# A mixture-of-experts block on one core: weights read in longer pieces, a different assignment of hidden units, and one buffer moved between two stages

## The chip, the cores and the metric

The kernel runs on one core of one Trainium2 chip. Times are device microseconds of one execution. Three runs of the kernel before took 1500.37, 1500.58 and 1503.2 us; the median is 1500.58 us. In the texts PE is TensorE, PEld its weight load, DVE VectorE, ACT ScalarE, POOL GpSimd, SP SyncE (which issues the weight transfers).

## The reference, cut to what matters

One decoder block on 512 tokens of 1024 channels. A recurrence and a windowed attention come first; their sum goes through an output projection. The part that the change touches follows:

```python
x = x + g1 * (merged @ w_out)                       # output projection and residual
h2 = rms_norm(x, norm2_gain) * (1 + sc2) + sh2
x = x + g2 * moe_ffn(h2, ...)                       # 32 experts, each token goes to 4

# per expert e, for the tokens xb that chose it
hu = xb @ w_up[e] + b_up[e]                         # w_up[e]: 1024 x 2048
x_glu = minimum(hu[:, ::2], 7)                      # even columns
x_lin = clip(hu[:, 1::2], -7, 7)                    # odd columns
act = x_glu * sigmoid(1.702 * x_glu) * (x_lin + 1)
y = act @ w_down[e] + b_down[e]                     # w_down[e]: 1024 x 1024
```

All is float32. Hidden unit h of an expert comes from columns 2h and 2h+1 of w_up and meets row h of w_down.

## The kernel before, in words

**Precision.** Matrix products run in float16 with each weight split into a high part (scaled and rounded, written by ACT in line 341) and a low part (what is left, computed by DVE in line 346), and three matmuls per product (high x high, low x high, high x low). A split takes a tile of 128 x 2048 float32 from a staging slot and writes two float16 halves into another slot.

**The slots.** All weights pass through a ring of slots, each 8 KB per partition. `NS` = 9 stand from the start (named slot). When the output projection begins, `NSB` = 5 more come (slotb); when the experts begin, and the projection's own tiles are given back, `NSC` = 4 more (slotc). A free slot is taken either by `pump`, which issues the next weight transfer on SP in a fixed order, or by `hl_take` for the output of a split. `free` and `hl_give` put slots back and pump again. The low part of a split is the last reader of a staged tile, so it decides when a weight slot comes free.

**The experts.** For each of 32 experts the ring brings eight tiles of w_up (`q_up`, rows 128k to 128k+127, 8 KB per row) and four of w_down (`q_dn`: 256 rows as two blocks of 128, so that one partition receives rows p and 128+p, 4 KB each). The eight up tiles and three of the four down tiles are split; the last down tile is used as float32. `split_up` reads the up tile with `p (f g) -> p g f`, g = 2: all even columns, then all odd ones, so that the innermost step of the read is 2 elements (8 bytes). The halves are written contiguously. `up_k` then takes 16 blocks of 128 columns (8 of the gated part, 8 of the linear part), each three matmuls against the gathered tokens `xg` of one k. `swiglu` forms the activation, `down_j` multiplies it with the down tiles, `finish` scales by gate and adds the rows to the output by an indirect DMA on POOL.

**Order.** In the expert loop the instructions of PE, ACT and DVE stay in the order in which they are written. `ahead(i)` issues the splits up to `LOOK` = 6 tiles ahead of the one being multiplied, as long as slots are free. Work of expert e's down product, expert e+1's up product and expert e+2's gather is woven together.

**The output projection.** For each of four tiles of 128 tokens, `logits` computes the projection, adds it to the residual input `x1`, forms the router's logits and writes x1 out (a DMA issued on POOL, line 983). Before, all four x1 tiles have a buffer of their own and are loaded on ACT's queue ahead of the loop (line 945).

**The table.** `overflow_table` computes how many experts got more tokens than one pass takes, and which; the loop behind the experts (line 1401) uses it and runs no pass here. Before, it is issued as one piece in the last turn of the expert loop.

Of the kernel before, what the change touches and what calls it, by code (L numbers as in the profile page):

```python
# [23 lines left out]
NT = 4  # L24
# [17 lines left out]
def block_body(tc, x, c, positions, w_ada, b_ada, norm1_gain, w_in, lower_bound_logits, hg_norm_gain,  # L42
# [19 lines left out]
    with top:  # L62
# [41 lines left out]
        def dview(ap, off, dims):  # L104
            return bass.AP(tensor=ap.tensor, offset=ap.offset + off, ap=dims)
# [54 lines left out]

        def q_dn(e, j):
            queue(("dn", e, j), lambda t: SP.dma_start(
                t.rearrange("p (k f) -> p k f", k=2),
                dview(w_down, (e * 1024 + 256 * j) * 1024, [[1024, 128], [128 * 1024, 2], [1, 1024]])))

        for g in range(4):
            q_ada1(g, 0)
# [772 lines left out]

        x1s, xas, rss = {}, {}, {}

        for t in range(NT):
            x1s[t] = wk.tile([128, D], F32, name=f"x1_{t}")
            A.dma_start(x1s[t], x2[128 * t:128 * t + 128, :])

        def logits(t, pieces):
# [92 lines left out]

        def bias_up():
            st = ready.pop(("bup",))
            src = st[:32, :].rearrange("p (f g) -> p g f", g=2)
            bk = sd_bank()
            for m in range(16):
                T.transpose(bk[:, 32 * m:32 * m + 32], src[:, m // 8, 128 * (m % 8):128 * (m % 8) + 128],
                            ident[:32, :32])
            A.activation(bu.rearrange("p e m -> p m e"), bk.rearrange("p (m e) -> p m e", m=16), AF.Copy, scale=SU)
            free(st)

# [4 lines left out]
            free(st)  # L1055

        def split_up(e, k, later=None):
            split(("up", e, k), 2048, later=later, view_in=lambda t: t.rearrange("p (f g) -> p g f", g=2),
                  view_hi=lambda t: t.rearrange("p (g f) -> p g f", g=2))

        order = []
        for e in range(NEX + 1):
# [25 lines left out]
        def select0(t0, t1):  # L1088
            V.tensor_tensor(sel0[:, t0:t1], iota_c[:, None, :C].to_broadcast([128, t1 - t0, C]),
                            pos[:, t0:t1, 0:1].to_broadcast([128, t1 - t0, C]), op=OP.is_equal)  # L1090

        for t in range(NT):
            if t == NT - 1:
                select0(0, NT - 1)
            logits(t, ((0, D),) if t < NT - 1 else LAST)
            pre(t + 1)
            if t < NT - 1:
                choose(t)
                make_h2(t)
                gates(t)  # L1100
# [84 lines left out]

        def up_k(hl, k, xg):
            for f in range(16):
                o = pu[f // 4][:, C * (f % 4):C * (f % 4) + C]
                for n, (pa_, pw) in enumerate(PASSES):
                    T.matmul(o, lhsT=hl[:, 2048 * pw + 128 * f:2048 * pw + 128 * f + 128], rhs=xg[:, pa_, k, :],  # L1190
                             start=False, stop=(k == KT - 1 and n == 2), skip_group_check=True)

        def swiglu(act, act32, read=None):
# [61 lines left out]

        NB = 32

        def overflow_table():

            cb = pse.tile([128, 512], F32, name="gb", bufs=2)  # L1260
            for t in range(NT):
                T.matmul(cb[:, :NE], lhsT=onesb, rhs=Mb[:, t, :], start=(t == 0), stop=(t == NT - 1))
            cnt = moe.tile([128, NE], F32, name="cnt")
            V.tensor_copy(cnt, cb[:, :NE])
            nbk = moe.tile([128, NE], F32, name="nbk")
            V.tensor_scalar(nbk, cnt, float(C), None, op0=OP.is_gt)
            q = 2
            while C * q < S:
                V.scalar_tensor_tensor(nbk, cnt, float(C * q), nbk, op0=OP.is_gt, op1=OP.add)
                q += 1  # L1270
            cum = moe.tile([128, NE], F32, name="cum")
            one_e = moe.tile([128, NE], F32, name="one_e")
            V.memset(one_e, 1.0)
            V.tensor_tensor_scan(cum, one_e, nbk, 0.0, op0=OP.mult, op1=OP.add)
            nblk = moe.tile([128, 2], I32, name="nblk")
            V.tensor_copy(nblk[:, 0:1], cum[:, NE - 1:NE])
            slot = hl_take()[0]
            cmpt = slot[:, :NB * NE].rearrange("p (b e) -> p b e", b=NB)
            V.tensor_tensor(cmpt, iota_c[:, :NB, None].to_broadcast([128, NB, NE]),
                            cum[:, None, :].to_broadcast([128, NB, NE]), op=OP.is_gt)  # L1280
            eix = moe.tile([128, NB], F32, name="eix")
            V.tensor_reduce(eix, cmpt, axis=AX.X, op=OP.add)
            eixi = moe.tile([128, NB], I32, name="eixi")
            V.tensor_scalar(eix, eix, float(NE - 1), None, op0=OP.min)
            V.tensor_copy(eixi, eix)
            beg = moe.tile([128, NB], F32, name="beg")

            V.tensor_sub(cum, cum, nbk)
            V.tensor_tensor(cmpt, iota_e[:, None, :].to_broadcast([128, NB, NE]),
                            eix[:, :, None].to_broadcast([128, NB, NE]), op=OP.is_equal)  # L1290
            V.tensor_mul(cmpt, cmpt, cum[:, None, :].to_broadcast([128, NB, NE]))
            V.tensor_reduce(beg, cmpt, axis=AX.X, op=OP.add)
            V.tensor_sub(beg, iota_c[:, :NB], beg)
            V.tensor_scalar(beg, beg, float(C), None, op0=OP.mult)
            hl_give(slot)
            return nblk, eix, eixi, beg

        def aux_of(e):
            return lambda t: aux[:, t, e, :]
# [29 lines left out]
        def rest():  # L1329

            for b in range(4):
# [2 lines left out]
                        next(prep, None)  # L1334
                up_bias(bu[:, 1], b)

        i = 0
        for e in range(NEX + 1):
            if e < NEX:
                prep = nexts.pop(e + 1, iter(()))  # L1340
                xg = state[e][0]
                for k in range(8):
                    ahead(i)
                    if e > 0 and k in PICK_AT:
                        next(prep, None)
                    up_k(hlmap[("up", e, k)], k, xg)
                    hl_done(("up", e, k))
                    i += 1
                    if e == 0 and k == 4:
                        for t in range(NT):  # L1350
                            T.matmul(gbs[3][:C, 4 * C:4 * C + 3], lhsT=sel0[:, t, :], rhs=aux[:, t, 0, :], start=False,
                                     stop=(t == NT - 1), skip_group_check=True)
                        slots_of(gbs[3][:C, 4 * C:4 * C + 3], gate, idx)
                        hl_give(sel0slot)
                        A.activation(gate[:, 3:4], bu[:, 0, 0:1], AF.Silu)
                lows = []
                ahead(i, lows)
                acts[e] = new_act()
                swiglu(*acts[e], read=rest if e == 0 else None)
                for low in lows:  # L1360
                    low()
                for _ in prep:
                    pass
                if e + 2 < NEX:
                    nexts[e + 2] = prepare(e + 2)
                    next(nexts[e + 2])
            if e == NEX:
                tables = overflow_table()
            if e > 0:
                _, gate, idx = state.pop(e - 1)  # L1370
                down_bias(E64[:, e - 1:e])
                for j in range(4):
                    ahead(i)
                    key = ("dn", e - 1, j)
                    if j < 2 and e < NEX - 1:
                        up_bias(bu[:, e + 1], 2 * j)
                        up_bias(bu[:, e + 1], 2 * j + 1)
                    if j >= 3:
                        down_j(ready[key], j, *acts[e - 1])
                        free(ready.pop(key))  # L1380
                    else:
                        down_j(hlmap[key], j, *acts[e - 1])
                        hl_done(key)
                    i += 1
                finish(gate, idx)
                acts.pop(e - 1)
# [14 lines left out]
        with tc.For_i(0, nreg, 1) as it:  # L1401
# [27 lines left out]
            for k in range(8):  # L1429
# [1 line left out]
                free_slots.rotate(-1)  # L1431
                SP.dma_start(stt, wup[ds(er, 1)].rearrange("o k f -> (o k) f")[128 * k:128 * k + 128, :])
                slot, hl = hl_take()
                src = stt.rearrange("p (f g) -> p g f", g=2)
                hi, lo = (hl[:, :2048].rearrange("p (g f) -> p g f", g=2),
                          hl[:, 2048:].rearrange("p (g f) -> p g f", g=2))
                A.activation(hi, src, AF.Copy, scale=SW)
                V.scalar_tensor_tensor(lo, src, SW, hi, op0=OP.mult, op1=OP.subtract)
                up_k(hl, k, xg)
# [5 lines left out]
            for j in range(4):  # L1445
                stt = free_slots[0]
                free_slots.rotate(-1)
                SP.dma_start(stt.rearrange("p (k f) -> p k f", k=2),
                             wdn[ds(er, 1)].rearrange("o (j k p) f -> p (o j) k f", j=4, k=2)[:, j])
                if j >= 3:  # L1450
                    down_j(stt, j, act, act32)
                    continue
# [9 lines left out]
        'w_hg_branch', 'q_norm_gain', 'k_norm_gain', 'attn_sinks', 'w_attn_branch', 'w_out', 'norm2_gain',  # L1462
        'w_router', 'b_router', 'w_up', 'b_up', 'w_down', 'b_down']
_OUTS = [((1, 512, 1024), 'float32')]
NSB, NSC = 5, 4
LOOK = 6
NHX = 6
SW_AT = {0: 1, 1: 2, 2: 2, 5: 4, 6: 3, 7: 3, 8: 3, 9: 3, 10: 3, 11: 3, 12: 3, 13: 3}
HG_AT = {9: 1, 10: 1, 11: 1, 12: 1, 13: 1, 14: 1, 15: 1, 16: 1, 17: 1}
# [25 lines left out]
```

## Time and profile before

| | us |
|---|---|
| median of three runs | 1500.58 |
| the profiled execution, its own time | 1501.85 |
| its span in the trace | 1500.1 |
| PE, DVE, ACT busy | 1402.3, 1299.1, 1053.5 |
| the experts, from the first up product to the last | 447 to 1463 |
| output projection | about 380 to 447 |

The profile is of one execution. Busy shares are averages over unlike stages, so the stage of the experts, two thirds of the span, is read by itself. A row that groups instructions gives their count, their busy time in total and the mean of one; a row of a stretch gives each engine's busy time in it, the granted TensorE clock (1.00 is full speed), the share of time that the 16 DMA engines were busy, and their rate.

### The profile page before, as it was taken

Reading aid. Unit: us, or ns where it says so; the run is one execution under the profiler, and the core shown is the slowest. Engines: PE = TensorE matmul, PEld = TensorE weight load, DVE = VectorE, ACT = ScalarE, POOL = GpSimd, SP = SyncE. Lnnn points to the kernel's source line nnn. Section 1 sums busy time; section 2 is a strip of 40 time slices with the busy share of each in tenths; the row PEclk is TensorE's granted clock in tenths of the full one; section 3 lists DMA queues with packets and bytes.
Section 4 is the critical chain, followed back from the end, with each engine's and each line's share of the span. In section 5 each row is a group of like instructions: output and inputs, shape, how many; then the busy total and the mean of one; then the engine's idle time right before and its main releaser. Section 6 shows DMA issues by size and latency. Waiting matters only on the chain. (4 is left out here: it accounts for less than half of the span.)

```text
span 1500.1 us, 41126 instructions
## 1 busy us (share of the span) xinstructions
PE 1402.3 (93%) x18200; PEld 1035.1 (69%) x18200; DVE 1299.1 (87%) x1457; ACT 1053.5 (70%) x1024; POOL 358.4 (24%) x82
## 2 busy tenths in 40 slices
PE   3979999999977999999999999999999999999994
PEld 2536567444557887788877888777887777888771
DVE  6876677777898999999999999999998899999885
ACT  4555424622548888888888888888887888888770
POOL 1020000010110233312433344203344333344400
PEclk9999999999989999999999999999999999999997
DMA  9832321376758999999999999999999999999971
GB/s 314 266 97 85 113 56 57 130 251 239 289 213 312 372 397 404 406 403 402 410 396 408 409 404 410 387 403 396 397 408 385 402 384 407 390 397 408 386 291 18
DMA packets 113521, 476.44 MB, mean 318 GB/s; under 512 B 10718, under 2 KB 35387, under 8 KB 80539
## 3 DMA queue, kind: packets, MB, share of 16 engines
q1 hardware_dynamic: 106160, 458.78, 77.8%
q0 software_dynamic: 5440, 12.72, 3.9%
q8 instruction: 144, 2.36, 0.6%
q10 hardware_dynamic: 1738, 2.27, 0.4%
q14 instruction: 39, 0.31, 0.1%
HBM read 463.22 MB, written 14.70 MB: 319 GB/s over the span
## 5 line engine op out<-in xcount | busy, mean ns | idle before, releaser
L1245 POOL DMA_INDIRECT out_dram<-y,idx x32 | 325.1, 10159 | 725.0 <-DVE y L1253 685.1
L1190 PE MATMUL pu<-xg,slot 128*128 128x96 f16 x10224 | 463.2, 206 | 10.5 <-issue 7.0
L1190 PEld LDWEIGHTS <-slot 128*128 128x128 f16 x10224 | 446.0, 98 | 28.6 <-issue 23.7
L346 DVE SCALAR_TENSOR_TENSOR slot<-slot,slot 128x2048 f16<-128x2048 f32 (+1 forms) x120 | 271.4, 2271 | 37.2 <-ACT slot L341 36.9
L341 ACT ACTIVATE slot<-slot 128x2048 f16<-128x2048 f32 (+1 forms) x120 | 242.2, 2031 | 79.1 <-DVE slot L346 24.6
L346 DVE SCALAR_TENSOR_TENSOR slot<-slotb,slot 128x2048 f16<-128x2048 f32 x101 | 227.7, 2282 | 8.2 <-ACT slot L341 7.9
L346 DVE SCALAR_TENSOR_TENSOR slot<-slotc,slot 128x2048 f16<-128x2048 f32 x97 | 219.7, 2283 | 12.6 <-ACT slot L341 12.4
L341 ACT ACTIVATE slot<-slotc 128x2048 f16<-128x2048 f32 x97 | 201.5, 2104 | 31.4 <-DMA slotc<-in_w_up_dram 9.9
L1241 PEld LDWEIGHTS <-act 128*96 128x96 f16 x1152 | 140.4, 124 | 115.5 <-issue 16.0
L341 ACT ACTIVATE slot<-slotb 128x2048 f16<-128x2048 f32 x101 | 197.4, 1957 | 32.0 <-PE pu L1190 11.4
L1241 PE MATMUL pd<-slot,act 128*96 128x512 f16 x924 | 206.4, 380 | 0.0
L701 PE MATMUL mm<-hT,slot 128*128 128x512 f16 x672 | 151.4, 381 | 0.0
L701 PEld LDWEIGHTS <-slot 128*128 128x128 f16 x672 | 65.5, 98 | 77.8 <-issue 2.9
L1150 PE MATMUL gb<-sel,h 128*128 128x96 f16 x1984 | 106.3, 208 | 11.7 <-ACT xg L1157 8.0
L1150 PEld LDWEIGHTS <-h 128*128 128x128 f16 x1984 | 92.4, 98 | 12.4 <-issue 10.3
L1190 PE MATMUL pu<-xg,slotb 128*128 128x96 f16 x2064 | 95.8, 206 | 4.2 <-issue 2.3
L1190 PEld LDWEIGHTS <-slotb 128*128 128x128 f16 x2064 | 90.7, 98 | 8.1 <-issue 7.1
L785 POOL DMA_DIRECT2D mdram<-mr x8 | 4.7, 591 | 270.0 <-DVE mr L779 207.0
L1233 PE MATMUL pd<-slot,act 128*96 128x512 f32 x144 | 64.7, 592 | 0.0
L1157 ACT ACTIVATE xg<-gb 128x384 f16<-128x384 f32 x124 | 59.1, 477 | 1.6 <-PE gb L1150 1.4
L1183 ACT ACTIVATE pu<-bu 128x384 f32<-128x384 f32 x128 | 57.0, 477 | 0.0
L346 DVE SCALAR_TENSOR_TENSOR slotb<-slot,slotb 128x2048 f16<-128x2048 f32 x20 | 45.8, 2289 | 11.6 <-ACT slotb L341 11.5
(339 smaller groups left out, 1634.9 us busy)
## 6 DMA issues: line engine op xcount, KB each, us to landing
slotc<-in_w_up_dram SPq DMA_DIRECT2D x116, 1024.0 KB, 19.4
slot<-in_w_up_dram SPq DMA_DIRECT2D x110, 1024.0 KB, 18.1
slotb<-in_w_down_dram SPq DMA_DIRECT2D x98, 1024.0 KB, 21.6
slotb<-in_w_up_dram SPq DMA_DIRECT2D x30, 1024.0 KB, 16.7
slot<-in_w_down_dram SPq DMA_DIRECT2D x20, 1024.0 KB, 22.5
slot<-in_w_in_dram SPq DMA_DIRECT2D x16, 1024.0 KB, 5.3
slot<-in_w_ada_dram SPq DMA_DIRECT2D x16, 1024.0 KB, 5.4
slotc<-in_w_down_dram SPq DMA_DIRECT2D x10, 1024.0 KB
```

Of the source, the lines that this page charges most:

```text
L341: A.activation(hi, src, AF.Copy, scale=SW)
L346: V.scalar_tensor_tensor(lo, src, SW, hi, op0=OP.mult, op1=OP.subtract)
L701: T.matmul(bk, lhsT=hl[:, o:o + 128], rhs=hT[:, ph, k, :], start=(k == 0 and n == 0), stop=(k == KT - 1 and n == 2))
L785: G.dma_start(mdram[q:q + 1, 512 * u:512 * u + 512], m)
L1150: T.matmul(bk[:, C * k:C * k + C], lhsT=h2[:, part, t, 128 * kk:128 * kk + 128], rhs=sel[:, t, :], start=(k == 0 and t == 0), stop=(t == N ...
L1157: A.activation(xg[:, part, 4 * u:4 * u + 4, :].rearrange("p k c -> p (k c)"), bk[:, :4 * C], AF.Copy)
L1183: A.activation(pu[i][:, :4 * C].rearrange("p (m c) -> p m c", m=4), b[:, 4 * i:4 * i + 4, None].to_broadcast([128, 4, C]), AF.Copy)
L1190: T.matmul(o, lhsT=hl[:, 2048 * pw + 128 * f:2048 * pw + 128 * f + 128], rhs=xg[:, pa_, k, :], start=False, stop=(k == KT - 1 and n == 2), ...
L1233: T.matmul(pd[u][:C, :], lhsT=act32[:, k - 4, :], rhs=w[:, o:o + 512], start=False, stop=(k == KT - 1))
L1241: T.matmul(pd[u][:C, :], lhsT=act[:, pa_, k, :], rhs=w[:, c0:c0 + 512], start=False, stop=False)
L1245: G.indirect_dma_start(out=out2, out_offset=bass.IndirectOffsetOnAxis(ap=idx[:n, :1], axis=0), in_=y[:n, :], in_offset=None, bounds_check= ...
```

## The change

1. `q_dn` reads 256 rows of w_down so that partition p receives rows 2p and 2p+1 of the block: one piece of 8 KB for each partition instead of two of 4 KB.
2. Hidden units must then meet these rows. The split of an up tile reads `p (f r) -> p r f` with r = 4: four passes of 512 elements, the innermost step being 4 elements (16 bytes). `up_k` picks its 128-column blocks accordingly, and so does `bias_up`.
3. x1 has two buffers. Tiles 0 and 1 are loaded ahead of their use as before; the load of tile t+1 is written ahead of the projection of tile t, on ACT's queue.
4. `NSB` goes from 5 to 6 and `NSC` from 4 to 3: one slot is there from the output projection on instead of from the experts on.
5. The table is a generator in three pieces, run in the turns of experts 6, 8 and 10 behind k = 3; each of the two later pieces borrows a ring slot while it runs.
6. In the first and the last turn with an up product, splits are no longer issued ahead between the up product and swiglu.

```diff
         def q_dn(e, j):
             queue(("dn", e, j), lambda t: SP.dma_start(
-                t.rearrange("p (k f) -> p k f", k=2),
-                dview(w_down, (e * 1024 + 256 * j) * 1024, [[1024, 128], [128 * 1024, 2], [1, 1024]])))
+                t, dview(w_down, (e * 1024 + 256 * j) * 1024, [[2048, 128], [1, 2048]])))
...
-        for t in range(NT):
-            x1s[t] = wk.tile([128, D], F32, name=f"x1_{t}")
+        def load_x1(t):
+            x1s[t] = wk.tile([128, D], F32, name="x1", bufs=2)
             A.dma_start(x1s[t], x2[128 * t:128 * t + 128, :])
...
         def split_up(e, k, later=None):
-            split(("up", e, k), 2048, later=later, view_in=lambda t: t.rearrange("p (f g) -> p g f", g=2),
-                  view_hi=lambda t: t.rearrange("p (g f) -> p g f", g=2))
+            split(("up", e, k), 2048, later=later, view_in=lambda t: t.rearrange("p (f r) -> p r f", r=4),
+                  view_hi=lambda t: t.rearrange("p (r f) -> p r f", r=4))
...
+        load_x1(0)
         for t in range(NT):
             if t == NT - 1:
                 select0(0, NT - 1)
+            if t < NT - 1:
+                load_x1(t + 1)
             logits(t, ((0, D),) if t < NT - 1 else LAST)
...
         def up_k(hl, k, xg):
             for f in range(16):
+                cb = 512 * (2 * (f % 2) + f // 8) + 128 * (f % 8 // 2)
                 o = pu[f // 4][:, C * (f % 4):C * (f % 4) + C]
                 for n, (pa_, pw) in enumerate(PASSES):
-                    T.matmul(o, lhsT=hl[:, 2048 * pw + 128 * f:2048 * pw + 128 * f + 128], rhs=xg[:, pa_, k, :],
+                    T.matmul(o, lhsT=hl[:, 2048 * pw + cb:2048 * pw + cb + 128], rhs=xg[:, pa_, k, :],
...
                     up_k(hlmap[("up", e, k)], k, xg)
                     hl_done(("up", e, k))
+                    if k == 3 and e in TABLE_AT:
+                        next(table)
...
                 lows = []
-                ahead(i, lows)
+                if 0 < e < NEX - 1:
+                    ahead(i, lows)
...
-            if e == NEX:
-                tables = overflow_table()
...
-NSB, NSC = 5, 4
+NSB, NSC = 6, 3
 LOOK = 6
+TABLE_AT = (6, 8, 10)
```

The order of instructions moves in two places that the prediction speaks of. The first is ACT in the output projection. Before, where `x_1_2862` to `x_3_2866` are the residual tiles of t = 1 to 3, ACT has no load among its work here:

```order
L1021 ACTIVATE gt,gs<-gt 128x4
L971 ACTIVATE xat<-sd 128x512
L963 ACTIVATE sqt,rs<-x_1_2862 128x1024
L971 ACTIVATE xat<-sd 128x512
L1004 ACTIVATE h_2220<-xa 128x1024
L1021 ACTIVATE gt,gs<-gt 128x4
```

Now, with `x_2899` the tile of t = 1 and `x_3170` that of t = 3 (lines are one lower):

```order
L1020 ACTIVATE gt,gs<-gt 128x4
L962 ACTIVATE sqt,rs<-x_2899 128x1024
L970 ACTIVATE xat<-sd 128x512 x2
L944 DMA x_3170<-in_x_dram 128x1024
L1003 ACTIVATE h_2220<-xa 128x1024
L1020 ACTIVATE gt,gs<-gt 128x4
```

The load of the fourth tile now stands in ACT's stream between the transposes' evictions of tile 1 and the cast of its h2; it waits for the write-out of tile 1, whose buffer it takes.

The second place is DVE behind the last split (`slot_71` before, `slot_64` now). Before, the table stands between the result of expert 30 and that of expert 31:

```order
L346 SCALAR_TENSOR_TENSOR slot_71<-slotc_3544,slot_71 128x2048
L1253 SCALAR_TENSOR_TENSOR y<-pd_3469,gate,g2row 96x512
L1253 SCALAR_TENSOR_TENSOR y<-pd_3470,gate,g2row 96x512
L1264 COPY cnt<-gb 128x32
L1266 TENSOR_SCALAR nbk<-cnt 128x32
L1269 SCALAR_TENSOR_TENSOR nbk<-cnt,nbk 128x32 x4
```

Now the two results stand one behind the other:

```order
L345 SCALAR_TENSOR_TENSOR slot_64<-slot_70,slot_64 128x2048
L1256 SCALAR_TENSOR_TENSOR y<-pd_3471,gate,g2row 96x512
L1256 SCALAR_TENSOR_TENSOR y<-pd_3472,gate,g2row 96x512
L1256 SCALAR_TENSOR_TENSOR y<-pd_3471,gate,g2row 96x512
L1256 SCALAR_TENSOR_TENSOR y<-pd_3472,gate,g2row 96x512
```

The table's instructions have left the end of DVE's stream; the same instructions stand in the turns of experts 6, 8 and 10.

## Rows read from the trace of the kernel before

**Rows 1.** The head of the page: busy time and share of each engine

```profile
PE 1402.3 (93%) x18200; PEld 1035.1 (69%) x18200; DVE 1299.1 (87%) x1457; ACT 1053.5 (70%) x1024; POOL 358.4 (24%) x82
```

**Rows 2.** Busy time by stretch: length, then each engine, TensorE clock, DMA share, GB/s

```profile
447.00:1463.00 1016.00, 988.90 (x15823) 799.79 (x15823) 950.35 (x790) 851.07 (x729) 322.25 (x30) 1.00 0.99 392
500.00:1440.00 940.00, 923.00 (x14603) 741.22 (x14601) 885.87 (x737) 791.61 (x679) 320.83 (x29) 1.00 1.01 399
```

**Rows 3.** What the weight queue waited for: us in total, times, longest

```profile
SPq L158 <- DVE slot L346: 258.6, 111, 8.1
```

**Rows 4.** DMA issues, from the page: KB each, us from issue to landing

```profile
slotc<-in_w_up_dram SPq DMA_DIRECT2D x116, 1024.0 KB, 19.4
...
slotb<-in_w_down_dram SPq DMA_DIRECT2D x98, 1024.0 KB, 21.6
```

**Rows 5.** Lines by form on DVE, low half of a split: busy us, mean ns, idle before

```profile
L346 DVE SCALAR_TENSOR_TENSOR slot<-slotb,slot 128x2048 f16<-128x2048 f32 x101 | 227.7, 2282 | 8.2 <-ACT slot L341 7.9
L346 DVE SCALAR_TENSOR_TENSOR slot<-slotc,slot 128x2048 f16<-128x2048 f32 x97 | 219.7, 2283 | 12.6 <-ACT slot L341 12.4
```

**Rows 6.** Lines by form on ACT, high half of a split

```profile
L341 ACT ACTIVATE slot<-slotc 128x2048 f16<-128x2048 f32 x97 | 201.5, 2104 | 31.4 <-DMA slotc<-in_w_up_dram 9.9 <-ACT slot L341 7.3 <-issue 6.3
L341 ACT ACTIVATE slot<-slotb 128x2048 f16<-128x2048 f32 x101 | 197.4, 1957 | 32.0 <-PE pu L1190 11.4 <-DMA slotb<-in_w_down_dram 8.7 <-DMA slotb<-in_w_up_dram 6.0
```

**Rows 7.** Lines by form on DVE: line 635 by length, and a sum of contiguous rows

```profile
L635 DVE TENSOR_TENSOR hf<-hf 128x512 f32<-128x512 f32 x2 | 1.4, 688 | 0.0
...
L635 DVE TENSOR_TENSOR hf<-hf 128x256 f32<-128x256 f32 x2 | 1.2, 624 | 0.0
...
L960 DVE TENSOR_TENSOR x<-x,xa 128x256 f32<-128x256 f32 x2 | 0.8, 414 | 0.0
```

**Rows 8.** Lines by form on DVE: one-operand reductions

```profile
L555 DVE TENSOR_REDUCE sst<-scores 128x8 f32<-128x2048 f32 x3 | 6.9, 2284 | 0.1
...
L1025 DVE TENSOR_REDUCE ge<-oh 128x32 f32<-128x128 f32 x4 | 1.5, 365 | 0.0
...
L1282 DVE TENSOR_REDUCE eix<-slotb 128x32 f32<-128x1024 f32 x1 | 1.2, 1220 | 0.0
```

**Rows 9.** Lines by form on ACT: two evictions of 512 elements

```profile
L971 ACT ACTIVATE xat<-sd 128x512 f16<-128x512 f32 x7 | 4.2, 597 | 8.9 <-PE sd L968 8.9
...
L1048 ACT ACTIVATE bu<-sd 128x512 f32<-128x512 f32 x1 | 1.0, 1033 | 4.9 <-PE sd L1046 4.9
```

**Rows 10.** Timeline of the end: start us, us, engine, line, operation, idle before

```profile
1471.63 0.17 DVE L1264 COPY cnt<-gb 128x32 f32<-128x32 f32 x1
...
1480.23 0.18 DVE L1294 TENSOR_SCALAR beg<-beg 128x32 f32<-128x32 f32 x1
...
1484.45 0.75 DVE L1253 SCALAR_TENSOR_TENSOR y<-pd,gate,g2row 96x512 f32<-96x512 f32 x1 [4.04 <-PE pd L1233]
```

**Rows 11.** Timeline of the output projection: writes of two tiles, and one ACT row

```profile
392.55 0.55 POOL L983 DMA_DIRECT2D out_dram<-x  x1 [9.45 <-DVE x L960]
...
410.70 0.56 POOL L983 DMA_DIRECT2D out_dram<-x  x1 [3.33 <-DVE gt L1023]
...
416.44 1.06 ACT L1004 ACTIVATE h<-xa 128x1024 f16<-128x1024 f32 x1 [3.77 <-DVE xa L1003]
```

**Rows 12.** DMA issues: those writes

```profile
out_dram<-x POOLq DMA_DIRECT2D x4, 512.0 KB, 6.3
```

**Rows 13.** Busy time in stretches of 2 us

```profile
438.00:440.00 2.00, 1.19 (x8) 0.60 (x8) 1.50 (x10) 0.59 (x3) 0.47 (x1) 0.50 0.99 418
474.00:476.00 2.00, 2.00 (x29) 2.00 (x27) 1.54 (x4) 1.28 (x3) 0.00 (x0) 0.50 0.80 324
482.00:484.00 2.00, 1.38 (x33) 1.38 (x34) 2.00 (x3) 1.77 (x2) 0.00 (x0) 1.00 0.42 86
```

**Rows 14.** Timeline of PE: the same gather at two clocks

```profile
463.64 1.52 PE L1150 MATMUL gb<-sel,h 128*128 128x96 f16 x32
473.16 2.72 PE L1150 MATMUL gb<-sel,h 128*128 128x96 f16 x32 [8.00 <-ACT xg L1157]
```

More of the change, by code (lines that the diff above doesn't have):

```diff
@@ L1042, in bias_up @@
             st = ready.pop(("bup",))
-            src = st[:32, :].rearrange("p (f g) -> p g f", g=2)
+            src = st[:32, :].rearrange("p (f r) -> p r f", r=4)
             bk = sd_bank()
             for m in range(16):
-                T.transpose(bk[:, 32 * m:32 * m + 32], src[:, m // 8, 128 * (m % 8):128 * (m % 8) + 128],
-                            ident[:32, :32])
+                k = m % 8
+                T.transpose(bk[:, 32 * m:32 * m + 32], src[:, 2 * (k % 2) + m // 8, 128 * (k // 2):128 * (k // 2) + 128], ident[:32, :32])
             A.activation(bu.rearrange("p e m -> p m e"), bk.rearrange("p (m e) -> p m e", m=16), AF.Copy, scale=SU)
@@ L1256, in block_body @@
         NB = 32
+        tables = []
         def overflow_table():
@@ L1276, in overflow_table @@
             V.tensor_copy(nblk[:, 0:1], cum[:, NE - 1:NE])
+            yield
             slot = hl_take()[0]
@@ L1282, in overflow_table @@
             V.tensor_reduce(eix, cmpt, axis=AX.X, op=OP.add)
+            hl_give(slot)
             eixi = moe.tile([128, NB], I32, name="eixi")
@@ L1288, in overflow_table @@
             V.tensor_sub(cum, cum, nbk)
+            yield
+            slot = hl_take()[0]
+            cmpt = slot[:, :NB * NE].rearrange("p (b e) -> p b e", b=NB)
             V.tensor_tensor(cmpt, iota_e[:, None, :].to_broadcast([128, NB, NE]),
@@ L1295, in overflow_table @@
             hl_give(slot)
-            return nblk, eix, eixi, beg
+            tables.extend((nblk, eix, eixi, beg))
+            yield
         def aux_of(e):
@@ L1335, in rest @@
                 up_bias(bu[:, 1], b)
+        table = overflow_table()
         i = 0
@@ L1433, in block_body @@
                 slot, hl = hl_take()
-                src = stt.rearrange("p (f g) -> p g f", g=2)
-                hi, lo = (hl[:, :2048].rearrange("p (g f) -> p g f", g=2),
-                          hl[:, 2048:].rearrange("p (g f) -> p g f", g=2))
+                src = stt.rearrange("p (f r) -> p r f", r=4)
+                hi, lo = (hl[:, :2048].rearrange("p (r f) -> p r f", r=4),
+                          hl[:, 2048:].rearrange("p (r f) -> p r f", r=4))
                 A.activation(hi, src, AF.Copy, scale=SW)
@@ L1448, in block_body @@
                 SP.dma_start(stt.rearrange("p (k f) -> p k f", k=2),
-                             wdn[ds(er, 1)].rearrange("o (j k p) f -> p (o j) k f", j=4, k=2)[:, j])
+                             wdn[ds(er, 1)].rearrange("o (j p k) f -> p (o j) k f", j=4, k=2)[:, j])
                 if j >= 3:
```

## The prediction

> **What bounds the kernel now.** I read the page's head first: PE is busy for 93% of the span and DVE for 87% [rows 1]. Such averages hide the stages, so the busy time by stretch came next. In the experts, 447 to 1463, three resources stand close together: PE 988.9 of 1016 us, DVE 950.35, the DMA engines at a share of 0.99; ACT has 851.07 [rows 2]. In the middle of it the DMA share is 1.01 at 399 GB/s. The reader is to see there that the weights' transfers are the bound, with PE 27 us and DVE 66 us behind it, and that nothing that adds to DVE has more than these 66 us of cover. The queue's own waits say how the parts hang together: the weight queue waited 258.6 us for slots that the low half of a split on DVE frees [rows 3]. A slower split is therefore not beside the chain; it hands out the slots. The DMA rows show both kinds of weight tile landing about 20 us after issue, 19.4 us for up and 21.6 us for down, which is a full queue and not the time of one tile [rows 4].
>
> **The split with a step of 16 bytes.** This edit decides the sum. The number and size of the splits stay: 32 experts x 8 up tiles = 256 splits, 2048 elements each. What changes is that each element read stands 4 elements after the one before, where it was 2. The low half now takes 2.28 us [rows 5], from tiles that are mostly up (slotc) and mostly down (slotb) alike: on DVE a step of 8 bytes costs nothing against a contiguous read. No split of before reads at 16 bytes, but line 635 does. It multiplies single elements at a step of 2s elements, for s = 1, 2, 4 and on. With 512 elements at 8 bytes it takes 688 ns; with only 256, at 16 bytes, 624 ns; a sum of 256 contiguous elements takes 414 ns [rows 7]. The inner extent is one element in both forms of line 635, so the step is what differs. The price is (624 - 414)/256 = 0.82 ns per element, or 1.68 us for 2048. That row has its step on both inputs and on the output, while the split has it on one input only. A row with one stepped input is the reduction of line 1025, at a step of 128 bytes: 365 ns for 128 elements. Contiguous reductions take 1220 ns for 1024 and 2284 ns for 2048 [rows 8], so 1.039 ns per element, and 128 would take 1220 - 896 x 1.039 = 289 ns. The price is 76/128 = 0.59 ns, or 1.22 us for 2048. Between 1.22 and 1.68 I take the middle, 1.45 us: the split shares its step with the one row and its single stepped input with the other. A low half would then take 3.73 us. A price of nothing is a rival below; below nothing I see no reason to go, as a contiguous read and one at 8 bytes already cost DVE the same.
>
> [...]
>
> ACT's high half reads the same view. It already pays for the step of 8 bytes: 2104 ns from slotc, mostly up tiles, against 1957 ns from slotb, mostly down [rows 6]. The only ACT row with a wider step is the eviction of line 1048, which writes at 64 bytes: 1033 ns for 512 elements where a contiguous one takes 597 ns [rows 9], so 0.85 ns per element or 1.74 us for 2048. ACT's high half lies then between 2.10 us (no more than now) and 1.96 + 1.74 = 3.70 us, an addition of 0 to 1.60 us. At the upper end ACT would be busy 851 + 256 x 1.60 = 1261 us. DVE comes to 950 + 256 x 1.45 = 1321 us: DVE sets the stage at my value, and ACT's addition lies beside it. It would be the bound only if DVE paid less.
>
> **The other edits.** The table: from its first instruction at 1471.63 to the last at 1480.23 + 0.18 it is 8.8 us of DVE. At the end it was beside PE's work: behind it DVE waited 4.04 us more for PE [rows 10]. Taking it away there gains nothing, while in the turns of experts 6, 8 and 10 it adds 8.8 us to the engine that will be the bound. Each of the later pieces holds one slot for a part of these 8.8 us; with transfers no longer the bound I set that to 0.
>
> The down tiles in pieces of 8 KB: the same bytes. If they moved faster, by 27 us at most since PE has no more idle time than that [rows 2], it would be for nothing once DVE takes 1300 us and the DMA engines have a quarter of that free. The sixth slotb lets one tile be loaded earlier, 1.05 MB at 399 GB/s = 2.6 us, again on a resource that no longer bounds: 0 taken, -2.6 as the other end.
>
> x1 in two buffers: the load of tile 2 waits for tile 0 to be written out. The write is issued at 392.55 and such writes land after 6.3 us [rows 11, 12], at 399, long before tile 2 is wanted. Behind the load of tile 3, ACT has the cast of h2 and the gates of tile 1, then the next evictions. Tile 1's write goes out at 410.70 and lands at 417.0, while the cast began at 416.44: 0.6 us late by the median, and at most the whole landing, 6.3 us. POOL and, further on, the router's chain wait behind that cast. I take 2 us, ends 0 and 6.3.
>
> Splits no longer issued ahead in the first and the last turn: two tiles' splits start a few us later, at the two places where DVE has to fill or drain anyway; 0, at most one low half, 3.7 us.
>
> **The sum.** In the stretch 447 to 1463 DVE has 950.35 + 371 + 8.8 = 1330 us of work. Of the 66 us that it idles now, part is waiting for transfers and will go, part is waiting for ACT's half and for PE at swiglu and will stay; I keep half, 33 us. The stretch becomes 1363 us, 347 more. Against the profiled execution's own 1501.85 us (1.75 us more than its span, and 1.27 more than the median of the runs) that is 1501.85 + 347 + 2 = 1851, at the level of the median 1850 us. Its own range: with 1.22 us per split and all idle time gone, 950 + 312 + 9 = 1271, so 1757 us; with 1.68 us and all of it kept, 950 + 430 + 9 + 66 = 1455, and 6 us for x1, so 1947 us.
>
> **The rivals.** *The step costs the split nothing.* For it speaks that DVE did not notice the step of 8 bytes; against it line 635, which did not notice 8 bytes either and paid at 16. Then transfers stay the bound, the table hides in DVE's 66 us, and what is gained is the slot's 2.6 us and what pieces of 8 KB save, between 0 and the 27 us that PE is idle. I take 4 us of these: 1500.6 - 6.6 + 0.6 for x1, 1495 us. This is the case on the other side; it decides from a price below 66/256 = 0.26 us per split, where DVE's cover ends. [...]
>
> *The step costs, but less in a split than in either row*, because this operation is limited by something else at 1.04 ns per element: a price of 0.6 us gives 950 + 154 + 9 + 50 = 1163, 1650 us. No row speaks for it; ACT would be the bound if its own price were high.
>
> [...]
>
> **How the numbers follow.** The forecast, 1850 us, has a chance of 0.77; no cost at all 0.10; the small price 0.07; the clock 0.06. The range of 1757 to 1947 leaves out the three rivals; I widen it to 1745 to 1950 for the terms set to 0. A change of less than 0.2%, 3 us, can't be told from none. Of the case without a cost, 0.07 are faster than that, 0.02 the same and 0.01 slower, if the borrowed slots or x1 take the gain. Slower in all: 0.77 + 0.07 + 0.06 + 0.01 = 0.91.
>
> **What would show it.** The row of the low half by form: splits of up tiles near 3.7 us, those of down tiles still at 2.28 us. In the experts DVE busy above 95% and the DMA share near 0.75. The queue's waits for DVE's splits grown several times. ACT's high half on up tiles anywhere from 2.1 to 3.7 us. At the end DVE's two results one behind the other, with the end no earlier. The prediction is wrong if up splits stay at 2.3 us, whatever the total says; if they do rise and the total does not, the cover that I read off DVE was larger than 66 us.

## The result and the profile after

The change makes the kernel slower by about a quarter: 1900.12 us, median of four runs (1898.98 to 1901.21), where the kernel before took 1500.62 us beside it (1500.37 to 1503.2). The ratio is 1.2657, with a 95% interval of 1.2639 to 1.2675. The forecast was 1850 us, 50 us too low, and the time lies inside the range of 1745 to 1950.

The head of the page of the kernel after, as in [rows 1]:

```profile
PE 1520.8 (80%) x18200; PEld 1144.2 (60%) x18200; DVE 1700.5 (90%) x1457; ACT 1500.7 (79%) x1024; POOL 562.6 (30%) x82
```

DVE is now the busiest engine. It has as many instructions as before (1457) and 401.4 us more work. ACT has the same 1024 instructions and 447.2 us more. Spread over the 256 up splits, both totals come to 1.57 us per low half and 1.75 us per high half. No number of instructions changed, so the same ones became longer.

Busy time of the kernel after in its up products, with the columns of [rows 2] (length, PE, PEld, DVE, ACT, POOL, granted clock, DMA share, GB/s). The row runs from the start of the first up product to the end of the last; the 447 to 1463 of [rows 2] reaches 11 us further, into the last down product:

```profile
455.70:1854.00 1398.30, 1095.69 (x15789) 903.47 (x15787) 1347.63 (x806) 1287.55 (x728) 527.56 (x30) 0.89 0.79 284
```

The same stretch of the up products in the kernel before:

```profile
446.70:1451.70 1005.00, 977.86 (x15785) 794.14 (x15782) 943.17 (x787) 846.21 (x727) 322.25 (x30) 1.00 1.00 395
```

The reader is to see three things here. DVE is busy for 96% of the stretch, where it was 94%. The DMA share fell from 1.00 to 0.79, so the transfers no longer bound it. And the difference of the spans, 1899.2 - 1500.1 = 399.1 us, divides cleanly: the first up product starts 9.0 us later, the stretch is 393.3 us longer (DVE has 404.5 us more work and is idle for 50.7 us instead of 61.8), and the tail behind it is 45.2 us instead of 48.4.

Lines by form on DVE in the kernel after, which answer to [rows 5]; the columns are the busy time, the mean ns of one, and the idle time before them:

```profile
L345 DVE SCALAR_TENSOR_TENSOR slot<-slotb,slot 128x2048 f16<-128x2048 f32 x123 | 352.1, 2898 | 10.2 <-ACT slot L340 10.2
L345 DVE SCALAR_TENSOR_TENSOR slot<-slotc,slot 128x2048 f16<-128x2048 f32 x73 | 280.5, 3868 | 8.3 <-ACT slot L340 8.3
...
L1256 DVE SCALAR_TENSOR_TENSOR y<-pd,gate,g2row 96x512 f32<-96x512 f32 x64 | 44.8, 741 | 13.5 <-PE pd L1236 13.5
```

The row from slotc holds up tiles alone: 3868 ns, where it was 2283. The row from slotb mixes both kinds, and its mean lies between. The other DVE operation shown kept its length.

The same view on ACT, which answers to [rows 6]:

```profile
L340 ACT ACTIVATE slot<-slotb 128x2048 f16<-128x2048 f32 x123 | 327.1, 2684 | 17.6 <-DVE beg L1302 9.0 <-DVE eix L1288 7.7 <-PE pu L1193 0.7
L340 ACT ACTIVATE slot<-slotc 128x2048 f16<-128x2048 f32 x73 | 283.5, 3921 | 2.5 <-PE pu L1193 2.5
```

The high half takes 3921 ns where it took 2104, above the 3.7 us that the prediction allowed, and two new releasers stand in the upper row: eix and beg, the table's reductions on DVE, 16.7 us together.

The weight queue's waits and the DMA issues, which answer to [rows 3] and [rows 4]:

```profile
SPq L158 <- DVE slot L345: 751.8, 176, 11.9
```

```profile
slotb<-in_w_down_dram SPq DMA_DIRECT2D x103, 1024.0 KB, 7.1
slotc<-in_w_up_dram SPq DMA_DIRECT2D x89, 1024.0 KB, 5.9
```

The queue waits almost three times as long for DVE, and a tile lands 6 to 7 us after its issue, where it took 19 to 22: hardly anything stands ahead of it in the queue any more.

### The profile page after: what moved, and what is told of

Same layout as the page of the kernel before. It is cut to its first block, busy times and chain, and to the rows that moved or that the text cites. A ratio compares the mean times of both kernels' runs of the same rounds, so it can differ in the third digit from the quotient of the medians.

```text
span 1899.2 us, 41104 instructions
## 1 busy us (share of the span) xinstructions
PE 1520.8 (80%) x18200; PEld 1144.2 (60%) x18200; DVE 1700.5 (90%) x1457; ACT 1500.7 (79%) x1024; POOL 562.6 (30%) x82
## 5 line engine op out<-in xcount | busy, mean ns | idle before, releaser
L1248 POOL DMA_INDIRECT out_dram<-y,idx x32 | 530.4, 16575 | 911.7 <-DVE y L1256 898.1
L1193 PE MATMUL pu<-xg,slot 128*128 128x96 f16 x10176 | 538.9, 221 | 118.2 <-ACT pu L1185 115.3
L1193 PEld LDWEIGHTS <-slot 128*128 128x128 f16 x10176 | 521.7, 107 | 140.1 <-issue 134.0
L340 ACT ACTIVATE slot<-slot 128x2048 f16<-128x2048 f32 (+1 forms) x121 | 412.3, 3428 | 49.8 <-DVE slot L345 25.3
L345 DVE SCALAR_TENSOR_TENSOR slot<-slot,slot 128x2048 f16<-128x2048 f32 (+1 forms) x121 | 419.6, 3476 | 35.8 <-ACT slot L340 34.4
L345 DVE SCALAR_TENSOR_TENSOR slot<-slotb,slot 128x2048 f16<-128x2048 f32 x123 | 352.1, 2898 | 10.2 <-ACT slot L340 10.2
L340 ACT ACTIVATE slot<-slotb 128x2048 f16<-128x2048 f32 x123 | 327.1, 2684 | 17.6 <-DVE beg L1302 9.0
L345 DVE SCALAR_TENSOR_TENSOR slot<-slotc,slot 128x2048 f16<-128x2048 f32 x73 | 280.5, 3868 | 8.3 <-ACT slot L340 8.3
L340 ACT ACTIVATE slot<-slotc 128x2048 f16<-128x2048 f32 x73 | 283.5, 3921 | 2.5 <-PE pu L1193 2.5
L700 PEld LDWEIGHTS <-slot 128*128 128x128 f16 x672 | 65.7, 98 | 77.7 <-issue 3.2
L340 ACT ACTIVATE slotb<-slot 128x2048 f16<-128x2048 f32 x21 | 78.4, 3739 | 0.0
L345 DVE SCALAR_TENSOR_TENSOR slotb<-slotb,slotb 128x2048 f16<-128x2048 f32 x24 | 69.2, 2884 | 2.4 <-ACT slotb L340 2.4
```

The lines of the kernel that those rows point to most:

```text
L700: T.matmul(bk, lhsT=hl[:, o:o + 128], rhs=hT[:, ph, k, :], start=(k == 0 and n == 0), stop=(k == KT - 1 and n == 2))
L1193: T.matmul(o, lhsT=hl[:, 2048 * pw + cb:2048 * pw + cb + 128], rhs=xg[:, pa_, k, :], start=False, stop=(k == KT - 1 and n == 2), skip_grou ...
L1248: G.indirect_dma_start(out=out2, out_offset=bass.IndirectOffsetOnAxis(ap=idx[:n, :1], axis=0), in_=y[:n, :], in_offset=None, bounds_check= ...
```

## The experiments

All times are beside runs of the kernel before on the same chip, whose medians were 1500.0 to 1501.7 us. The edits are against the kernel after, unless it says against before.

**The step without the step: weights read with a step by TensorE.** One kernel undoes parts 1 and 2 (the 8 KB pieces and the new assignment of hidden units). Another keeps them but puts the splits back to a step of 8 bytes; its edit is this:

```diff
-            split(("up", e, k), 2048, later=later, view_in=lambda t: t.rearrange("p (f r) -> p r f", r=4),
-                  view_hi=lambda t: t.rearrange("p (r f) -> p r f", r=4))
+            split(("up", e, k), 2048, later=later, view_in=lambda t: t.rearrange("p (f g) -> p g f", g=2),
+                  view_hi=lambda t: t.rearrange("p (g f) -> p g f", g=2))
...
-                cb = 512 * (2 * (f % 2) + f // 8) + 128 * (f % 8 // 2)
+                cb = 1024 * (f // 8) + 256 * (f % 8 // 2) + f % 2
...
-                    T.matmul(o, lhsT=hl[:, 2048 * pw + cb:2048 * pw + cb + 128], rhs=xg[:, pa_, k, :],
+                    T.matmul(o, lhsT=hl[:, 2048 * pw + cb:2048 * pw + cb + 255:2], rhs=xg[:, pa_, k, :],
```

The expectation for the kernel with parts 1 and 2 undone:

> The kernel after with parts 1 and 2 undone (down tiles again in pieces of 4 KB, the up split again at a step of 8 bytes); x1 in two buffers, the slot moved and the table in three pieces stay. Theory A (the 16-byte step of the split is the whole loss): 1495 to 1504 us, low half of every split 2.28 us. Rival B (the borrowed slots, the later loads of x1 or the splits no longer issued ahead cost tens of us too): 1515 us or more.

For the one above, in which TensorE picks every second float16 of the split tile as it loads weights:

> The kernel after, but the split reads at a step of 8 bytes again and the weights are picked for the up product with a step of two float16 elements (4 bytes), so that the down tiles still come in pieces of 8 KB. Theory A with a weight load that does not notice a step of 4 bytes: 1485 to 1503 us, PE's weight load 98 ns as before. Rival C (the weight load pays for any step): a mean near 200 ns and PE as the bound, 1900 us or more.

For parts 1 and 2 alone, added to the kernel before:

> The kernel before with parts 1 and 2 alone. Theory A: 1885 to 1900 us, within 1% of the kernel after, low half of an up split 3.8 to 3.9 us, high half 3.9 us. Rival B: below 1880 us, the rest being due to the other parts.

Measured: with parts 1 and 2 undone 1504.11 us, ratio 1.0019 (1.0010 to 1.0028). By TensorE's step 1496.55 us, 0.9971 (0.9961 to 0.9981). Parts 1 and 2 alone 1880.27 us, 1.2524 (1.2504 to 1.2545). The first lies 0.1 us above its range; the last misses its range by 5 us, and the missing 20 us up to the kernel after are the table's (below). So these parts carry the loss, and within them the step at which the splits read. Lines by form in the kernel with TensorE's step, on DVE and on the weight load, and the weight load of the kernel before:

```profile
L345 DVE SCALAR_TENSOR_TENSOR slot<-slotc,slot 128x2048 f16<-128x2048 f32 x73 | 165.0, 2283 | 4.8 <-ACT slot L340 4.8
```

```profile
L1193 PEld LDWEIGHTS <-slot 128*128 128x128 f16 x10176 | 446.3, 98 | 24.8 <-issue 20.9 <-ACT slot L340 3.2 <-ACT slotb L340 0.5
```

```profile
L1190 PEld LDWEIGHTS <-slot 128*128 128x128 f16 x10224 | 446.0, 98 | 28.6 <-issue 23.7 <-ACT slot L341 2.9 <-ACT pu L1183 1.1
```

The same numbers reach TensorE in the same order, the split is back at 2283 ns, and the weight load takes 98 ns with the step as without: 4 bytes from element to element show no cost there.

**The split's price by itself.** A kernel that only splits one resident tile, ACT and DVE one after the other, with elements 1, 2, 3, 4 and 8 apart (4 to 32 bytes), each twice, and at the end with the view of the kernel after (four passes of 512 at 16 bytes):

> No part of the block is computed; the output is zeros. ACT's high half and DVE's low half of 2048 elements run one behind the other on tiles that stay in place, with the read at steps of 1, 2, 3, 4 and 8 elements (4, 8, 12, 16, 32 bytes), twice, and at the end with the view of the kernel after (four passes of 512 at 16 bytes). Theory A (the price is the engine's own, and comes with the share of elements that open a new 16-byte stretch): DVE 2.28, 2.28, somewhat more at 12 bytes, 3.8 to 3.9 us at 16, no more at 32; ACT 1.9, 2.1, more at 12, 3.9 at 16, the same at 32. Rival F (the price needs both engines on the same tile at once): both stay below 3 us at 16 bytes here.

The timeline of DVE in it (start, us, line, operation, and the wait before); the last row has the view of the kernel after:

```profile
26.56 2.29 DVE L35 SCALAR_TENSOR_TENSOR lo<-src,hi 128x2048 f16<-128x2048 f32 x1 [24.63 <-ACT hi L32]
30.93 2.29 DVE L35 SCALAR_TENSOR_TENSOR lo<-src,hi 128x2048 f16<-128x2048 f32 x1 [2.08 <-ACT hi L32]
36.19 2.87 DVE L35 SCALAR_TENSOR_TENSOR lo<-src,hi 128x2048 f16<-128x2048 f32 x1 [2.97 <-ACT hi L32]
42.92 3.75 DVE L35 SCALAR_TENSOR_TENSOR lo<-src,hi 128x2048 f16<-128x2048 f32 x1 [3.87 <-ACT hi L32]
50.60 3.82 DVE L35 SCALAR_TENSOR_TENSOR lo<-src,hi 128x2048 f16<-128x2048 f32 x1 [3.93 <-ACT hi L32]
...
88.12 3.75 DVE L54 SCALAR_TENSOR_TENSOR lo<-src,hi 128x2048 f16<-128x2048 f32 x1 [3.87 <-ACT hi L53]
```

The timeline of ACT in it, its halves of the same five steps:

```profile
24.62 1.91 ACT L32 ACTIVATE hi<-src 128x2048 f16<-128x2048 f32 x1 [22.60 <-DMA src<-in_w_up_dram]
28.88 2.01 ACT L32 ACTIVATE hi<-src 128x2048 f16<-128x2048 f32 x1 [2.36 <-DVE lo L35]
33.26 2.90 ACT L32 ACTIVATE hi<-src 128x2048 f16<-128x2048 f32 x1 [2.36 <-DVE lo L35]
39.09 3.80 ACT L32 ACTIVATE hi<-src 128x2048 f16<-128x2048 f32 x1 [2.93 <-DVE lo L35]
46.70 3.86 ACT L32 ACTIVATE hi<-src 128x2048 f16<-128x2048 f32 x1 [3.82 <-DVE lo L35]
```

Each engine pays alone, with the other at rest, so the price does not come from both reading the tile at once. From 8 to 16 bytes DVE pays 3.75 - 2.29 = 1.46 us and ACT 3.80 - 2.01 = 1.79 us; 32 bytes add 0.07 us on DVE and 0.06 on ACT. The four passes of the kernel after take 3.75 us like one pass at 16 bytes, so it is the step that costs. The prices lie up to 0.1 us below those expected. In the kernel after the low half takes 3.87 us and the high half 3.92, each 0.12 us more than here. On DVE 8 bytes cost nothing (2.29 us, as with 4), 12 bytes cost 0.58 us, 16 bytes cost 1.46 us. On ACT 8 bytes already cost 0.10 us.

**One engine at a time.** Of the two readers one went back to 8 bytes. In the first kernel ACT reads at 8 and DVE at 16 bytes; the second exchanges them. The halves then stand in different column orders.

```diff
-            A.activation(hi, src, AF.Copy, scale=SW)
+            osrc = src if other is None else other(st)
+            ohi = hi if other is None else hl[:, :n].rearrange("p (g f) -> p g f", g=2)
...
+            A.activation(ohi, osrc, AF.Copy, scale=SW)
...
+                  other=lambda t: t.rearrange("p (f g) -> p g f", g=2))
```

> The kernel after with ACT's high half of the up split back at a step of 8 bytes and DVE's low half left at 16 (the two halves then stand in different column orders, so the output is not the reference's). Theory A (DVE sets the stage of the experts and ACT's own addition lies beside it, as the prediction has it): DVE's low half stays near 3.87 us, 1860 to 1897 us. Rival E (the two engines hand each other the slots, so ACT's addition is a good part of the loss): below 1820 us. Rival F (DVE pays only because ACT reads the same lines at the same time): low half below 3.5 us.

> The mirror: DVE's low half back at a step of 8 bytes, ACT's high half left at 16 (again not the reference's output). Theory A: ACT becomes the bound; it has 851 + 256 x 1.75 = 1299 us in the experts, with some 50 us of waits 1350 us, so 1820 to 1865 us in all: nearly the whole loss again, because both engines would be the bound alone. Rival G (ACT can run ahead of DVE and its addition hides): below 1650 us.

Measured: DVE alone at 16 bytes 1856.9 us, 1.2377 (1.2358 to 1.2396); ACT alone 1807.81 us, 1.2052 (1.2034 to 1.2071). Busy time from the first up product to the end of the last, DVE alone, and then ACT alone:

```profile
450.80:1807.80 1357.00, 1069.81 (x15785) 870.54 (x15785) 1342.41 (x806) 832.75 (x728) 524.94 (x30) 0.91 0.81 292
```

```profile
451.50:1759.30 1307.80, 1036.62 (x15789) 849.33 (x15787) 966.80 (x806) 1282.72 (x727) 70.25 (x30) 0.92 0.82 303
```

With DVE alone, DVE is busy for 99% of it and ACT for 61%; with ACT alone it is 74% and 98%. So each engine sets the stage when it pays alone. Alone they cost 357 and 308 us, together 399: most of ACT's addition does lie beside DVE's, but about 42 us do not. Both times lie below the ranges expected, by 3 and by 12 us; of the 50 us of waits allowed for ACT alone, 25 came. That ACT's addition costs nothing beside DVE's is refuted by these 42 us. The waits of DVE for ACT show most of them (us in total, times, longest): in the kernel after, 43.8 us in these two rows,

```profile
DVE slot L345 <- ACT slot L340: 34.7, 33, 3.9
DVE slotb L345 <- ACT slotb L340: 9.1, 8, 2.7
```

and with DVE alone 7.9 us:

```profile
DVE slot L348 <- ACT slot L343: 7.0, 5, 2.1
DVE slotb L348 <- ACT slotb L343: 0.9, 1, 0.9
```

**The table.** The kernel after with the table in one piece at the end again, and the kernel before with the table in pieces:

```diff
-                    if k == 3 and e in TABLE_AT:
-                        next(table)
...
+            if e == NEX:
+                for _ in table:
+                    pass
```

> The kernel after with the table back in one piece at the end, all else as it is. Theory A (ACT's split waits 16.7 us for the two slots that the table's pieces borrow, and DVE does 8.8 us of table while it is the bound): 1878 to 1888 us. Rival H (the distance to the kernel with parts 1 and 2 alone comes from x1 and the slots): 1893 us or more.

> The kernel before with part 5 alone: the table in three pieces in the turns of experts 6, 8 and 10. Theory A (the table's borrowed slots make ACT's split wait, 11.7 us of such waits in the kernel without the interleave, of which DVE's cover hides most): 1501 to 1505 us, up to 4 us more than before. Rival J (the pieces cost nothing while transfers are the bound): within 1 us of before.

Measured: 1879.29 us, 1.2525 (1.2506 to 1.2544), for the one; 1501.61 us, 0.9998 (0.9987 to 1.0009), for the other. The first is the time of parts 1 and 2 alone. So the 20 us between that and the kernel after come with the table in pieces, which costs nothing where the transfers are the bound. Busy time from the first up product to the end of the last, with the table at the end, and a line by form on ACT:

```profile
453.40:1832.40 1379.00, 1090.36 (x15785) 897.87 (x15783) 1338.56 (x787) 1286.25 (x728) 549.93 (x30) 0.89 0.80 288
```

```profile
L340 ACT ACTIVATE slot<-slotb 128x2048 f16<-128x2048 f32 x123 | 327.6, 2690 | 0.2 <-PE mm L902 0.2
```

The waits for eix and beg are gone: 17.6 us of idle time became 0.2. In the kernel after ACT had stood behind the slots that the table borrows, and DVE behind ACT: the stretch is 19.3 us shorter with the table at the end, by 9.1 us of DVE's work and by 10.3 us that it is idle (40.4 instead of 50.7).

**The pieces of 8 KB, and the slots.** Two parts added to the kernel before by themselves: the longer pieces, and then x1 in two buffers with the sixth slotb and fewer splits ahead.

```diff
-                t.rearrange("p (k f) -> p k f", k=2),
-                dview(w_down, (e * 1024 + 256 * j) * 1024, [[1024, 128], [128 * 1024, 2], [1, 1024]])))
+                t, dview(w_down, (e * 1024 + 256 * j) * 1024, [[2048, 128], [1, 2048]])))
```

> The kernel before with the down tiles in pieces of 8 KB and nothing else; rows of w_down then meet other hidden units, so the output is not the reference's. It prices part 1 alone. Theory A: nothing measurable to 8 us less (1492 to 1501 us), as the transfers are the bound before and a piece has at most a small price. Rival D (pieces of 4 KB cost the queue several per cent): 1470 to 1490 us.

> The kernel before with parts 3, 4 and 6: x1 in two buffers, one slot moved from slotc to slotb, no splits ahead in the first and last turn; the table stays at the end. Theory A (these parts give nothing, as the ring is full either way): within 1.5 us of before. Rival K (the later loads of x1 cost the projection some us): 1502 us or more, with the first up product later than at 447 us; the tile loaded earlier could also give 2.6 us.

Measured: the pieces 1493.46 us, 0.9952 (0.9938 to 0.9966); the slots 1503.64 us, 1.0011 (1.0002 to 1.0020), some 2 us lost, as rival K had it. The DMA view from 600 to 1400 with longer pieces, and then before (packets, MB, and the weight queue's share of the 16 engines):

```profile
DMA packets 46202, 323.53 MB, mean 404 GB/s; under 512 B 6010, under 2 KB 6010, under 8 KB 7610
...
q1 hardware_dynamic: 43284, 315.20, 95.9%
```

```profile
DMA packets 58316, 320.36 MB, mean 400 GB/s; under 512 B 5962, under 2 KB 5962, under 8 KB 32659
...
q1 hardware_dynamic: 55400, 312.05, 96.0%
```

With 22% fewer packets the queue moves 1% more bytes in the same 800 us. That is 7 us of gain (0.0048 of 1500) while transfers are the bound. No run takes the pieces out of the kernel after, whose DMA share is 0.79; that they gain nothing there is argued and not shown.

**The best version.** From these follows the kernel before with 8 KB pieces and the new assignment through TensorE's step, and nothing else of the change:

> The kernel before with the down tiles in pieces of 8 KB and the hidden units assigned by picking weight columns at a step of two float16 elements; the split, x1, the slots and the table stay as before. Theory A (part 1 is worth about 7 us, parts 3 to 6 cost about 3): 1489 to 1497 us, below both kernels and below the version that keeps parts 3 to 6. Rival I (parts 3 to 6 do no harm once part 1 is there): the same as that version, 1496 to 1499 us.

Measured: 1493.74 us, 0.9951 (0.9937 to 0.9965). It is 0.5% faster than the kernel before, and its gain is that of the pieces alone. That it beats the version that keeps parts 3 to 6 (0.9961 to 0.9981) is not shown, as the intervals overlap.

## Why the prediction held, and where it was short

**Right: what bounds, and why.** The 16-byte step decides, DVE sets the stage (96% busy, "above 95%" was said), the DMA share falls to 0.79 ("near 0.75"), and the queue waits for DVE. Undoing the step at the splits alone takes the time from 1.2657 to 0.9971 of before. Up splits take 3.87 us; down splits stay near 2.3. The rival without a cost is refuted by the rows of the split, the one with 0.6 us too.

**The account of the 50 us.** In the span the forecast was +349 us (347 and 2 for x1), and 399 came. By its own terms:

- The price of the split, set to 1.45 us between two rows: it is 1.57 us per split in the kernel, +30 us over 256 splits, within the bounds of 1.22 and 1.68. By itself it is 1.46 us, what I had; that the middle of two other rows comes so close is luck. The remaining 0.1 us also stands with ACT at 8 bytes (3868 ns), so it is not ACT's step, and not the four passes either (3.75 us alone); where it comes from is open.
- The idle time of DVE: I let it fall by half, 33 us; it fell from 61.8 to 50.7 us, by 11. That is +22 us. The step that failed here is "ACT's addition lies beside it". ACT's high half grew by 1.75 us, above my upper end of 1.60, and both engines came near the bound. Two engines that hand each other every tile, at 96% and 92%, cost 42 us more than DVE alone. In the profiled executions it is 46 us: 5 at the front, 5 of DVE's work, and 36 that DVE is idle (50.7 instead of 14.6). With the table at the end DVE is still idle for 40.4 us. So about 26 of the 36 come with ACT's step whether the table is in pieces or not, and about 10 only with both.
- The borrowed slots, set to 0 because the transfers would have room: the table in pieces costs about 20 us in all, of which 8.8 were in the sum; 10 are idle time of DVE. I looked at the transfers into the slot and not at ACT, which waits for it ahead of DVE. This lies inside the idle time above and is not to be added to it.
- The front, set to +2: +9.0, so +7 us. Most of it comes with the 16-byte splits made ahead during the output projection, which I had not charged at all: with ACT back at 8 bytes the first up product starts at 450.76 instead of 455.73, and with parts 1 and 2 alone, without the x1 part, at 456.76. The shares are rough, since with the table at the end, which changes nothing up to there, it starts at 453.44.
- The rest, -9 us: DVE's work in the stretch grew by 404.5 us and not by the 410 of 256 splits and the table (-6), of which the low halves of three splits ahead of the first up product explain 5; and the tail is 3.2 us shorter (-3), which I had at 0.

30 + 22 + 7 - 9 = 50. That the idle time would stay could be seen in the trace of before: 53.8 of its 61.8 us are waits of DVE for ACT's half, the engine that the change slows too (us in total, times, longest):

```profile
DVE slot L346 <- ACT slot L341: 42.4, 73, 2.8
DVE slotb L346 <- ACT slotb L341: 11.4, 14, 3.0
```

The 2 us for x1 had about the right size by luck. The x1 part alone moves the first up product from 446.71 to 449.19, but not by the wait that the prediction named. There the cast of tile 1 starts at 416.82, where it was 416.44 [rows 11], and it waits for DVE and not for the load. The delay arises behind the last cast, where the first gather on PE now waits for the router's result of the last tile. Rows with the x1 part alone, on ACT and PE, and then PE in the kernel before:

```profile
416.82 1.06 ACT L1004 ACTIVATE h<-xa 128x1024 f16<-128x1024 f32 x1 [3.02 <-DVE xa L1003]
```

```profile
442.57 2.08 PE L1123 MATMUL gb<-slot,h 128*128 128x96 f16 x24 [1.65 <-DVE lg L982]
```

```profile
440.33 2.08 PE L1120 MATMUL gb<-slot,h 128*128 128x96 f16 x24
```

Why the gather waits there is open. The x1 tiles 0 and 1 are not loaded as before either: the loads are issued at 385.04 instead of 379.32, and DVE waits 3.69 us for tile 0, which is made up by the cast of tile 1.

The front of the kernel after can be seen on ACT. The timeline of the kernel after:

```profile
398.24 0.60 ACT L970 ACTIVATE xat<-sd 128x512 f16<-128x512 f32 x1 [0.63 <-PE sd L967]
400.81 3.89 ACT L340 ACTIVATE slot<-slot 128x2048 f16<-128x2048 f32 x1 [1.98 <-DVE slot L345]
404.59 0.60 ACT L970 ACTIVATE xat<-sd 128x512 f16<-128x512 f32 x1
...
411.65 1.06 ACT L1003 ACTIVATE h<-xa 128x1024 f16<-128x1024 f32 x1 [6.46 <-DVE xa L1002]
```

The kernel before, from the same place:

```profile
396.07 0.60 ACT L971 ACTIVATE xat<-sd 128x512 f16<-128x512 f32 x1 [1.87 <-PE sd L968]
...
400.97 2.09 ACT L341 ACTIVATE slot<-slot 128x2048 f16<-128x2048 f32 x1 [2.36 <-DVE slot L346]
402.96 1.05 ACT L1004 ACTIVATE h<-xa 128x1024 f16<-128x1024 f32 x1
```

The second eviction of tile 0 now stands behind a split of 3.89 us, which itself waits for a split on DVE, and starts at 404.59 instead of 396.07, and the first cast to h follows 8.7 us later than before.

**Right: the table at its old place.** Taking it from the end gains nothing: the tail behind the last up product is 45.2 us without it and 44.9 with the table put back there. DVE waits for PE instead. Before, it came from the table and waited 4.04 us for PE [rows 10]. Now its waits at y are these (us in total, times, longest):

```profile
DVE y L1256 <- PE pd L1236: 13.5, 2, 12.5
```

The 8.8 us of the table have turned into a wait of 12.5 us for the same product.

**Right: the clock.** The chance of 0.06 was for a clock that falls until PE is the bound; in the kernel before a gather took 2.72 us instead of 1.52 where the granted clock was 0.50 [rows 13, 14]. In the kernel after the clock fell, and did not decide. Busy time in stretches of 2 us in the kernel after:

```profile
628.00:630.00 2.00, 1.18 (x24) 1.07 (x24) 2.00 (x3) 2.00 (x3) 0.00 (x0) 1.00 1.04 410
630.00:632.00 2.00, 0.00 (x0) 0.00 (x0) 2.00 (x2) 2.00 (x1) 0.00 (x0) 0.59 0.27 115
632.00:634.00 2.00, 1.23 (x16) 1.22 (x16) 2.00 (x3) 2.00 (x4) 0.00 (x0) 0.50 0.33 74
```

PE stands still for 3.38 us behind one split of ACT's, the granted clock goes to 0.50, and PE starts on 16 matmuls with it. Over the stretch the clock is 0.89 and PE has 1095.7 us of work where it had 977.9, but the stretch is 1398 us long, so PE is busy for 78% of it and does not become the bound. PE's waits are named in the waits of the kernel after:

```profile
PE gb L1152 <- ACT xg L1159: 148.9, 39, 17.1
PE pu L1193 <- ACT pu L1185: 139.9, 58, 3.4
```

It hardly waits for splits (11 us in all at the up product) but for two short instructions of ACT, the gathered tokens (xg) and the bias that is written to pu. At 632 us the second of these stands behind a split of 3.83 us in ACT's order.

**Right in kind: the 8 KB pieces.** I had 4 us in the rival and 0 in the forecast. The 4 us were my estimate, and no run shows them: alone the pieces bring 7.2 us (5.1 to 9.3), more than the estimate and of the same order. In the kernel after the transfers have 21% to spare.

## What to carry to other kernels

When a new data layout is paid for by a stepped read, ask which engine reads with the step and how many bytes lie between elements: here 8 bytes cost DVE nothing (2.29 us) and 16 bytes cost 64% (3.75 us), while TensorE's weight load took 98 ns with a step of 4 bytes as without. Move the permutation to the reader that does not pay. And when two engines pass every tile to each other, price the slower one's addition and then ask how near the other comes to the bound: here, with ACT at 61%, DVE was idle for 15 us, and with ACT at 92% for 51, and a borrowed slot that cost nothing in the kernel before brought 10 of these.

## What was not expected

The prediction spoke of 8 and 16 bytes only. A step of 12 bytes already costs (2.87 us on DVE, 2.90 on ACT), and one of 32 hardly more than 16 (3.82 and 3.86 us), as the probe's expectation then had it. And POOL's indirect write of the results has another length in each of three kernels, in which DVE is busy for different shares of the stretch. Lines by form on POOL, before:

```profile
L1245 POOL DMA_INDIRECT out_dram<-y,idx x32 | 325.1, 10159 | 725.0 <-DVE y L1253 685.1 <-DVE cnt L1264 26.2 <-DVEq L1401 13.8
```

After:

```profile
L1248 POOL DMA_INDIRECT out_dram<-y,idx x32 | 530.4, 16575 | 911.7 <-DVE y L1256 898.1 <-DVEq L1414 13.6
```

And with ACT alone at 16 bytes:

```profile
L1252 POOL DMA_INDIRECT out_dram<-y,idx x32 | 73.1, 2284 | 1277.9 <-DVE y L1260 1265.3 <-DVEq L1418 12.6
```

The same 32 instructions take 10.2 us each with DVE at 94%, 16.6 with DVE at 96%, and 2.3 with DVE at 74%; with DVE at 99% they take 16.5. POOL is idle for hundreds of us beside them and no engine is seen to wait for it; spans on POOL are rough, and why it is so was not tried.
